# Scaling attention outputs instead of probabilities, with the inverse sums spread to rows by ScalarE and TensorE and the transposes copied by two engines

## The chip, the cores and the metric

The kernel runs on one core of a Trainium2 chip. The metric is the device time of one execution in microseconds (us). The core's engines work side by side, each through its own instructions in order: TensorE (PE, with its weight loads as PEld), VectorE (DVE), ScalarE (ACT), GpSimd (POOL) and SyncE (SP), which issues most DMAs. Matrix products and transposes are written to PSUM, from where another engine has to copy or read them.

## The reference

A trunk of two layers over 1024 tokens of 1024 features. Layer 0 mixes by a state-space scan and a convolution and is not touched. Layer 1 mixes by two kinds of attention, whose outputs are gated and multiplied by the output weights:

```python
def masked_softmax(s, mask):
    s = jnp.where(mask, s.astype(jnp.float32), NEG)
    m = jnp.max(s, axis=-1, keepdims=True)
    e = jnp.exp(s - m) * mask
    return e / jnp.maximum(jnp.sum(e, axis=-1, keepdims=True), 1e-30)
...
    p_c = masked_softmax(s_c, jnp.asarray(dist_c >= 0))
    o_cmp = jnp.einsum('bygsc,bcyd->bsygd', p_c, vc)
...
        o_sel = jnp.einsum('bygqk,byqkd->bqygd', p_s, vs)
...
        o_win = jnp.einsum('bygqk,bkyd->bqygd', p_w, vw)
...
    o = g[:, :, 0] * o_cmp + g[:, :, 1] * o_sel + g[:, :, 2] * o_win
```

This is NSA: 8 query heads on 2 key-value heads of 64 features, with three branches. The compressed branch attends to block averages (`vc` are their values), the selected branch to the blocks that rank highest by the compressed probabilities, the window branch to the last 512 tokens; `g` are sigmoid gates for each token, head and branch. MLA, the second kind, is ordinary causal attention of 8 heads of 64 value features with the same `masked_softmax`. Everything is in float32.

## The kernel before

Tokens lie in eight blocks `i` of 128 on the partitions. Layer 1 (`layer1`) goes through stages, of which three matter here. The order of the instructions on each engine is made by a scheduler from the code's data dependences and its own estimates, so that neighbouring loops overlap and an engine's order is not that of the code.

**Compression and gates.** `cmp_attn` (L1200) takes the compressed branch, block by block, in the free place `vslot` (`fr`): exponentials, sums, and at L1232 the probabilities times their gate, `pg`, into one of two places (by i % 2). TensorE transposes them (L1236), ScalarE copies them to `pcT` (L1238), and a DMA (L1239) stores `pcT` in `gp_dram`. For blocks 4 to 7 VectorE then ranks the key blocks (L1245 to L1261, a chain of small steps of which L1256 to L1260 each handle 128 x 512 elements), TensorE transposes the result (L1264), ScalarE casts it (L1267). In between run projections of the gates (`gate_proj`, products at L121, `th` at L1281 and L1282).

**NSA** (`nsa`, L1335). For each block, in the order 1, 2, 0, 3 to 7, and for each of two halves `gp` of four heads, first the window branch, then the selected branch: TensorE makes scores for 4, 2 or 1 heads at a time (L1385, mask, L1390) into one of two two-bank places `S`. `softmax_group` (L1286) takes the maximum (L1291, VectorE), the exponentials with their sums (L1294, ScalarE), the gate times the clamped inverse of the sums (L1300, L1301, VectorE), and multiplies the probabilities by it (L1303, VectorE). `transpose_group` (L1305) transposes them in 128 x 128 pieces, up to four into a PSUM bank (L1315), and ScalarE copies the bank to `PT` (L1316). The products with the values (L1405) of both branches, and that of `pcT` with `vc` (L1410), are summed in one bank `o`, the only one of its pool. `store_y` (L1326) multiplies it by the other gate (L1330).

**MLA** (`mla`, L1577) does the same for 16 steps of four heads: scores (L1603, L1606, L1607), `softmax_group`, `transpose_group` into `PTm`, products (L1615), `store_y`.

The float32 products appear in the trace as two records each, the transposes and the scores as one.

## Time and profile before

| | us |
|---|---|
| median of 3 runs | 1548.22 |
| lowest and highest | 1547.45, 1552.62 |
| profiled execution | 1549.67 |
| its span in the trace | 1547.9 |
| compression and gates | 807.7 to 921.5 |
| NSA | 921.5 to 1173.1 |
| MLA | 1173.1 to 1337.0 |

Over the span TensorE is busy for 1464.6 us (95%), VectorE for 962.6 (62%), ScalarE for 627.8 (41%), GpSimd for 375.4 (24%). Times in rows count from the start of the span. A row of the timeline gives the start, the length, and how many instructions of one kind follow one another (x8); records overlap, so the distance from one start to the next tells what an instruction costs. In brackets stands the idle time ahead of it and what ended that.

### The profile page before, as it was taken

Reading aid. Unit: us, or ns where it says so; the run is one execution under the profiler, and the core shown is the slowest. Engines: PE = TensorE matmul, PEld = TensorE weight load, DVE = VectorE, ACT = ScalarE, POOL = GpSimd, SP = SyncE. Lnnn points to the kernel's source line nnn. Section 1 sums busy time; section 2 is a strip of 40 time slices with the busy share of each in tenths; the row PEclk is TensorE's granted clock in tenths of the full one; section 3 lists DMA queues with packets and bytes.
Section 4 is the critical chain, followed back from the end, with each engine's and each line's share of the span. In section 5 each row is a group of like instructions: output and inputs, shape, how many; then the busy total and the mean of one; then the engine's idle time right before and its main releaser. Section 6 shows DMA issues by size and latency. Waiting matters only on the chain.

```text
span 1547.9 us, 22106 instructions
## 1 busy us (share of the span) xinstructions
PE 1464.6 (95%) x8284; PEld 1169.3 (76%) x8284; DVE 962.6 (62%) x1960; ACT 627.8 (41%) x1291; POOL 375.4 (24%) x334
## 2 busy tenths in 40 slices
PE   5879999989999999999999999999999999999998
PEld 4668878867787788789877776666666877787787
DVE  6799889968534655561386357787775676434322
ACT  4322312257213334431252237777665676312211
POOL 3369634331224201410321310010001100223400
PEclk8989999999999999999999999999999999999999
DMA  6232443323423422542833274221113241432422
GB/s 204 62 116 82 134 152 122 137 69 122 150 96 125 147 93 73 154 151 64 189 96 106 79 217 111 73 78 37 28 42 99 77 129 45 153 113 84 172 79 72
DMA packets 141475, 167.59 MB, mean 108 GB/s; under 512 B 20464, under 2 KB 108264, under 8 KB 141112
## 3 DMA queue, kind: packets, MB, share of 16 engines
q1 hardware_dynamic: 136440, 154.76, 32.5%
q0 software_dynamic: 4672, 11.39, 2.4%
q8 instruction: 66, 1.08, 0.3%
q14 instruction: 41, 0.34, 0.1%
q10 hardware_dynamic: 256, 0.03, 0.0%
HBM read 114.20 MB, written 49.94 MB: 106 GB/s over the span
## 4 chain that ended last, share of the span: by engine, by line
PE 74%; DVE 11%; ACT 4%; DMA 4%; issue 4%; POOL 2%; SPq 1%; ACTq 0%; DVEq 0%; POOLq 0%
PE S L121 41%; PE tr L1315 6%; PE tr L121 5%; PE o L1405 5%; PE o L1615 2%; PE S L1390 2%; PE S L1385 2%; PE S L1606 1%; PE S L1603 1%; PE S L1607 1%; DVE acc L544 1%; PE tr L849 1%; PE S L1320 1%; PE tr L1020 1%; DMA acc<-x 1%
## 5 line engine op out<-in xcount | busy, mean ns | idle before, releaser
L121 PE MATMUL S<-xT,wt 128*128 128x512 f32 x768 | 190.7, 402 | 12.3 <-DVE ext L267 10.0
L121 PE MATMUL S<-X,wt 128*128 128x512 f32 x768 | 183.6, 394 | 5.7 <-ACT wt L114 2.3
L121 PE MATMUL S<-wo,Y 128*128 128x512 f32 x768 | 181.7, 395 | 3.5 <-DVE gb L724 2.1
L121 PE MATMUL S<-wg,hT 128*128 128x512 f32 x720 | 173.6, 398 | 4.2 <-ACT wg L114 4.0
L121 PEld LDWEIGHTS S<-xT,wt 128*128 128x128 f32 x768 | 143.5, 191 | 44.2 <-DVE ext L267 10.5
L121 PEld LDWEIGHTS S<-wo,Y 128*128 128x128 f32 x768 | 143.6, 189 | 34.8 <-DVE gb L724 2.5
L121 PEld LDWEIGHTS S<-X,wt 128*128 128x128 f32 x768 | 141.8, 188 | 36.6 <-issue 3.7
L121 PEld LDWEIGHTS S<-wg,hT 128*128 128x128 f32 x720 | 134.9, 190 | 35.5 <-ACT wg L114 7.6
L1291 DVE TENSOR_REDUCE nm<-S 128x1 f32<-128x640 f32 (+7 forms) x132 | 128.9, 980 | 49.5 <-PE S L1390 30.1
L283 DVE SCALAR_TENSOR_TENSOR conv<-ext,conv 128x1024 f32<-128x1024 f32 x116 | 149.3, 1287 | 3.3
L115 POOL TENSOR_TENSOR wt<-raw,wt 128x1024 fp32r<-128x1024 f32 x34 | 84.2, 2492 | 99.8 <-ACT wt L114 99.6
L1294 ACT ACTIVATE pslot<-S,nm 128x640 f32<-128x640 f32 (+7 forms) x128 | 89.8, 708 | 31.7 <-DVE nm L1291 24.6
L1316 ACT COPY PT<-tr 128x512 f32<-128x512 f32 (+3 forms) x172 | 78.9, 492 | 40.9 <-PE tr L1315 36.1
L1405 PE MATMUL o<-PT,vslot 128*64 128x256 f32 x528 | 82.5, 391 | 0.4 <-ACT PT L1316 0.4
L1315 PE MATMUL tr<-ident,pslot 128*128 128x128 f32 x528 | 81.8, 283 | 0.0
L104 DVE TENSOR_SCALAR rs_v<-ss 128x1 f32<-128x1 f32 (+1 forms) x29 | 4.5, 154 | 116.9 <-ACT lh L100 102.3
L1315 PEld LDWEIGHTS tr<-ident,pslot 128*128 128x128 f32 x528 | 58.4, 142 | 24.9 <-issue 19.2
L1390 PE MATMUL S<-kst,qslot 112*128 112x512 f32 (+3 forms) x192 | 74.4, 400 | 0.0
L1385 PE MATMUL S<-kst,qslot 128*128 128x512 f32 (+3 forms) x192 | 70.3, 366 | 3.5 <-ACT pslot L1294 2.5
L834 POOL TENSOR_TENSOR lh<-lh 128x1024 f32<-128x1024 f32 x16 | 40.2, 2512 | 118.7 <-DVE lh L833 103.1
L100 ACT ACTIVATE lh<-S 128x1024 f32<-128x1024 f32 x16 | 16.4, 1027 | 125.6 <-issue 95.5
L899 DVE SCALAR_TENSOR_TENSOR ov<-ov,S 128x1024 f32<-128x1024 f32 (+1 forms) x17 | 19.7, 1158 | 72.6 <-issue 44.6
(452 smaller groups left out, 2759.2 us busy)
## 6 DMA issues: line engine op xcount, KB each, us to landing
h_dram<-lh POOLq DMA_DIRECT2D x16, 512.0 KB, 3.2
hr<-h_dram SPq DMA_DIRECT2D x14, 512.0 KB, 3.4
raw<-ev_w_in SPq DMA_DIRECT2D x16, 256.0 KB, 3.3
raw<-ev_w_in SPq DMA_DIRECT2D x8, 512.0 KB, 6.1
raw<-ev_w_out SPq DMA_DIRECT2D x8, 512.0 KB, 4.9
t<-ple_gate SPq DMA_DIRECT2D x8, 512.0 KB, 4.8
raw<-ple_gate SPq DMA_DIRECT2D x8, 512.0 KB, 4.4
lh<-x SPq DMA_DIRECT2D x8, 512.0 KB, 4.9
```

Source lines behind the costliest of these rows:

```text
L115: (eng or self.nc.gpsimd).tensor_tensor(lo, raw, hi, OP.subtract)
L121: self.nc.tensor.matmul(ps, l, r, start=n == 0, stop=n == len(seq) - 1)
L283: nc.vector.scalar_tensor_tensor(out=last if s == 30 else acc, in0=src, scalar=wc, in1=acc, op0=OP.mult, op1=OP.add)
L834: nc.gpsimd.tensor_tensor(hv, hv, xr, OP.add)
L1291: nc.vector.tensor_reduce(out=nm[:, 0:hg], in_=S[:, :, 0:n], op=OP.max, axis=AX.X, negate=True)
L1294: nc.scalar.activation(out=P[:, h, 0:n], in_=S[:, h, 0:n], func=AF.Exp, bias=nm[:, h:h + 1], accum_out=sm[:, h:h + 1])
L1315: nc.tensor.transpose(ps[:, c:c + 128], P[:, h, 128 * (k0 + k):128 * (k0 + k) + 128], self.ident)
L1316: nc.scalar.copy(PT[:, k0:k0 + n, s0:s0 + hg], ps[:, 0:128 * n * hg].rearrange("p (k h t) -> p k h t", h=hg, t=128))
L1385: nc.tensor.matmul(o_, QA[:, hd], KA[:, y, ks], start=True, stop=False)
L1390: nc.tensor.matmul(o_, qb[:, hd], KB[:, y, ks], start=False, stop=True)
L1405: nc.tensor.matmul(o[64 * y:64 * y + 64].rearrange("p g t -> p (g t)"), self.vsw[:, k0 + kt, 128 * br + 64 * y:128 * br + 64 * y + 64], PT ...
L1615: nc.tensor.matmul(o[64 * b:64 * b + 64, q], vm[:, kt, vs], PT[:, kt, 2 * b + q], start=(kt == 0), stop=(kt == nk - 1))
```

## The change

The probabilities are no longer scaled. `exp_group` is what is left of `softmax_group`: the maximum (L1297) and the exponentials (L1299), whose sums for all four heads of a branch go into one `sm`. The clamp, gate and inverse are made once for each branch and half (L1405, L1408) or MLA step, 48 times.

The inverse has to multiply the output, which has features on the partitions and tokens along a row. So `spread` (L1304, ScalarE) copies the four inverse sums to 64 columns each, and `inverse_rows` (L1309, TensorE) transposes that by two 128 x 128 transposes into PSUM; in NSA ScalarE copies the two branches' rows together to `f` (L1415). The two branches now have separate halves of the bank `o`; VectorE multiplies `o` by `f` (L1422), adds the branches (L1423) and adds the compressed output (L1424). In MLA the rows multiply the gate `sgm` in place (L1630), and `store_y` is as before.

The compressed branch is multiplied by its values in `cmp_attn` already (L1242, two products of 512 columns for each block). Its output `oc` is copied (L1244) into the place in which that block's `pg` was, and stored in `gp_dram` in place of `pcT` (L1245).

The copies of transposed probabilities (L1323) go alternately to ScalarE and VectorE: 132 and 126 of the 258.

```diff
+            ps = self.bank()
+            for y in range(2):
+                pr = slice(64 * y, 64 * y + 64)
+                nc.tensor.matmul(ps[pr], self.vc[pr], pcT[pr].rearrange("p g t -> p (g t)"), start=True, stop=True)
+            oc = fr[:, 4:8, 128 * (i % 2):128 * (i % 2) + 128]
+            nc.scalar.copy(oc, ps.rearrange("p (g t) -> p g t", g=4))
-            nc.sync.dma_start(self.gp_dram[i, :, 1], pcT)
+            nc.sync.dma_start(self.gp_dram[i, :, 1], oc)
...
-        nc.vector.reciprocal(r[:, 0:hg], r[:, 0:hg])
-        for h in range(hg):
-            nc.vector.tensor_scalar(out=P[:, h, 0:n], in0=P[:, h, 0:n], scalar1=r[:, h:h + 1], scalar2=None, op0=OP.mult)
+    def spread(self, r, dst):
+
+        self.nc.scalar.copy(dst, r.rearrange("p (a b o) -> p b a o", a=2, o=1).to_broadcast([128, 2, 2, 64]))
+
+    def inverse_rows(self, r, dst):
+
+        for b in range(2):
+            self.nc.tensor.transpose(dst[:, b], r[:, b].rearrange("p a e -> p (a e)"), self.ident)
...
-            nc.scalar.copy(PT[:, k0:k0 + n, s0:s0 + hg],
-                           ps[:, 0:128 * n * hg].rearrange("p (k h t) -> p k h t", h=hg, t=128))
+            copy = nc.vector.tensor_copy if (k0 // kb + s0 // hg) % 2 else nc.scalar.copy
+            copy(PT[:, k0:k0 + n, s0:s0 + hg], ps[:, 0:128 * n * hg].rearrange("p (k h t) -> p k h t", h=hg, t=128))
...
-                o = self.ps_o.tile([128, 2, 128], F32, tag="o", name="o")
+                o = self.ps_o.tile([128, 2, 2, 128], F32, tag="o", name="o")
+                r = self.t2([2, 2, 2, 64], name="inv")
...
+                    nc.vector.reciprocal(sm, sm)
+                    self.spread(sm, r[:, 1 - br])
+                    if br == 0:
+                        fp = self.bank().rearrange("p (b g t) -> p b g t", b=2, g=2)
+                        for b in range(2):
+                            self.inverse_rows(r[:, b], fp[:, b])
+                        f = self.t2([2, 2, 128], name="rows")
+                        nc.scalar.copy(f, fp)
...
-                for y in range(2):
-                    nc.tensor.matmul(o[64 * y:64 * y + 64].rearrange("p g t -> p (g t)"), self.vc[64 * y:64 * y + 64],
-                                     pcT[64 * y:64 * y + 64, 2 * gp:2 * gp + 2].rearrange("p g t -> p (g t)"),
-                                     start=False, stop=True, skip_group_check=True)
+                nc.vector.tensor_tensor(f, o, f, OP.mult)
+                nc.vector.tensor_tensor(f[:, 0], f[:, 0], f[:, 1], OP.add)
+                nc.vector.tensor_tensor(f[:, 0], f[:, 0], oc[:, 2 * gp:2 * gp + 2], OP.add)
...
+            f = self.bank()[:, 0:256].rearrange("p (g t) -> p g t", g=2)
+            self.inverse_rows(r, f)
+            nc.vector.tensor_tensor(sgm, f, sgm, OP.mult)
```

Three places show how the order on an engine changes. In the compression stage, TensorE's order around the first ranking transposition (L1264 before, L1270 after), for block 4; what stands in brackets is which engine or DMA queue an instruction waits for.

Before:

```order
L121 MATMUL S<-X_4494,wt 128x512 x4
L121 MATMUL S<-X_4495,wt 128x512 x4
L121 MATMUL S<-X_4494,wt 128x512 x2
L1264 MATMUL tr<-ident,pmv 16x128 [waits DVE_49,Activation_49]
L1264 MATMUL tr<-ident,pmv 16x128
L1236 MATMUL tr<-ident,vslot 128x128 [waits Activation_49]
L1236 MATMUL tr<-ident,vslot 128x128 x3
L121 MATMUL S<-X_4494,wt 128x512 x2
```

After:

```order
L121 MATMUL S<-X_4495,wt 128x512 x4
L1242 MATMUL tr<-pcT,vc 64x512 [waits Activation_49]
L1242 MATMUL tr<-pcT,vc 64x512
L1236 MATMUL tr<-ident,vslot 128x128 [waits DVE_49,PE_49]
L1236 MATMUL tr<-ident,vslot 128x128 x3
L1242 MATMUL tr<-pcT,vc 64x512 [waits Activation_49]
L1242 MATMUL tr<-pcT,vc 64x512
L1270 MATMUL tr<-ident,pmv 16x128 [waits DVE_49,PE_49]
L1270 MATMUL tr<-ident,pmv 16x128
L1236 MATMUL tr<-ident,vslot 128x128 [waits PE_49]
L1236 MATMUL tr<-ident,vslot 128x128 x3
L1242 MATMUL tr<-pcT,vc 64x512 [waits Activation_49]
```

The compressed products of blocks 3, 4 and 5 now stand around the transposition, that of block 4 right ahead of it, with no product of the gates between them.

VectorE's order at the same place, from the last ranking steps of block 4 (L1257 to L1261 before, L1263 to L1267 after).

Before:

```order
L1256 TENSOR_TENSOR E<-pmv 128x512 [waits DVE_49]
L1257 TENSOR_TENSOR E<-pmv 128x512
L1258 TENSOR_TENSOR E<-E,vslot 128x512 [waits DMAHW7_49,DVE_49]
L1259 TENSOR_TENSOR E<-E 128x512 [waits DVE_49]
L1260 TENSOR_REDUCE pmv<-E 128x32 [waits DVE_49]
L1261 TENSOR_SCALAR pmv<-pmv 128x32 [waits DVE_49]
L1232 TENSOR_TENSOR vslot<-E,cgt 128x2x4x64 [waits PE_49]
L1245 MEMSET pmv 128x2 [waits DVE_49]
```

After:

```order
L1263 TENSOR_TENSOR E<-pmv 128x512
L1232 TENSOR_TENSOR vslot<-E,cgt 128x2x4x64 [waits DMAHW0_49,Activation_49]
L1264 TENSOR_TENSOR E<-E,vslot 128x512 [waits DVE_49]
L1230 RECIPROCAL cgt<-ginv 128x8 [waits DVE_49]
L1232 TENSOR_TENSOR vslot<-E,cgt 128x2x4x64 [waits DMAHW1_49,Activation_49]
L1265 TENSOR_TENSOR E<-E 128x512 [waits DVE_49]
L1266 TENSOR_REDUCE pmv<-E 128x32 [waits DVE_49]
L1267 TENSOR_SCALAR pmv<-pmv 128x32 [waits DVE_49]
L1251 MEMSET pmv 128x2 [waits DVE_49,PE_49]
```

L1232 for blocks 5 and 6 stands inside the ranking of block 4, and waits for a DMA queue (that of `oc` of blocks 3 and 4) where it waited for TensorE.

TensorE's order at the start of NSA: before, from the second score tile's last head to the third's first; after, from the same head to the transposes of the first tile (`pslot`).

Before:

```order
L1385 MATMUL S<-kst,qslot 128x256
L1320 LDWEIGHTS mbf
L1320 MATMUL S<-mbf 128x128
L1390 MATMUL S<-kst,qslot 128x256
L1385 MATMUL S<-kst,qslot 128x256 [waits DVE_49,Activation_49]
```

After:

```order
L1326 MATMUL S<-mbf 128x128
L1399 MATMUL S<-kst,qslot 128x256
L1321 MATMUL tr<-ident,pslot 128x128 [waits Activation_49]
L1321 MATMUL tr<-ident,pslot 128x128
L1321 MATMUL tr<-ident,pslot 128x128 [waits Activation_49]
L1321 MATMUL tr<-ident,pslot 128x128
L1321 MATMUL tr<-ident,pslot 128x128 [waits Activation_49]
L1321 MATMUL tr<-ident,pslot 128x128
L1321 MATMUL tr<-ident,pslot 128x128 [waits Activation_49]
L1321 MATMUL tr<-ident,pslot 128x128
L1394 MATMUL S<-kst,qslot 128x256 [waits DVE_49]
```

The first tile's eight transposes, which followed the third score tile, now stand ahead of it, and each pair waits for its own exponential.

Over the whole order, runs of output products without another instruction between them become fewer: in NSA 74 (with the compressed products) become 64, in MLA 45 become 32, 26 of the latter with an odd number of products before and 20 after.

## Rows read from the trace of the kernel before

**Rows 1.** Windows: length, busy of PE, PEld, DVE, ACT, POOL, granted clock, DMA

```profile
807.70:921.50 113.80, 105.78 (x489) 86.26 (x488) 61.66 (x90) 28.64 (x45) 23.98 (x24) 1.00 0.42 125
921.50:1173.10 251.60, 247.78 (x1684) 164.66 (x1682) 181.81 (x425) 174.52 (x450) 16.33 (x29) 0.99 0.24 69
1173.10:1337.00 163.90, 159.34 (x1306) 126.39 (x1304) 107.83 (x233) 105.34 (x252) 12.40 (x10) 0.98 0.34 101
927.14:932.60 5.46, 5.46 (x25) 4.89 (x26) 3.79 (x13) 2.71 (x10) 0.37 (x2) 0.50 0.93 227
```

**Rows 2.** Waits of PE in NSA and MLA: total us, times, longest

```profile
PE S L1385 <- ACT pslot L1294: 2.5, 5, 1.4
PE S L1603 <- DVE sr L1301: 2.3, 1, 2.3
```

**Rows 3.** Groups by line: busy us, mean ns | idle before, releasers

```profile
L1303 DVE TENSOR_SCALAR pslot<-pslot,sr 128x640 f32<-128x640 f32 (+7 forms) x128 | 60.7, 500 | 2.9
L1315 PE MATMUL tr<-ident,pslot 128*128 128x128 f32 x528 | 81.8, 283 | 0.0
L1315 PEld LDWEIGHTS tr<-ident,pslot 128*128 128x128 f32 x528 | 58.4, 142 | 24.9 <-issue 19.2 <-ACT PT L1316 1.9 <-ACT pslot L1294 1.9
```

**Rows 4.** Timeline of PE in NSA: start, us, engine, line, operation

```profile
938.78 0.65 PE L1410 MATMUL o<-sgpc,vc 64*64 64x256 f32 x4
939.37 0.44 PE L1315 MATMUL tr<-ident,pslot 128*128 128x128 f32 x2
...
1017.74 0.65 PE L1405 MATMUL o<-PT,vslot 128*64 128x256 f32 x2
1018.32 0.76 PE L1315 MATMUL tr<-ident,pslot 128*128 128x128 f32 x5
```

**Rows 5.** Timeline of PE in MLA

```profile
1262.23 0.60 PE L1315 MATMUL tr<-ident,P 128*128 128x128 f32 x4
1262.76 1.09 PE L1615 MATMUL o<-PTm,vm 128*64 128x128 f32 x16
1263.79 0.44 PE L1603 MATMUL S<-KAm,qmslot 128*128 128x384 f32 x1
...
1268.98 0.66 PE L1615 MATMUL o<-PTm,vm 128*64 128x128 f32 x8
1269.57 0.87 PE L1315 MATMUL tr<-ident,P 128*128 128x128 f32 x6
1270.20 0.48 PE L1603 MATMUL S<-KAm,qmslot 128*128 128x512 f32 x1
```

**Rows 6.** Timeline of PE in compression and gates, waits in brackets

```profile
835.92 1.40 PE L121 MATMUL S<-X,wt 128*128 128x512 f32 x5 [1.59 <-DVE th L1282]
...
848.91 4.88 PE L121 MATMUL S<-X,wt 128*128 128x512 f32 x20 [1.14 <-ACT wt L114]
...
856.45 0.39 PE L1264 MATMUL tr<-ident,pmv 128*16 128x128 f32 x2 [2.65 <-DVE pmv L1261]
```

**Rows 7.** Timeline of DVE in the ranking of one block

```profile
845.32 1.07 DVE L1246 TENSOR_REDUCE pmv<-E 128x128 f32<-128x512 f32 x1 [5.15 <-issue]
...
849.05 2.89 DVE L1257 TENSOR_TENSOR E<-pmv 128x512 f32<-128x512 f32 x1
...
854.76 0.69 DVE L1259 TENSOR_TENSOR E<-E 128x512 f32<-128x512 f32 x1
```

**Rows 8.** Timeline of ACT behind a ranking transposition

```profile
845.31 0.57 ACT L1267 CAST sl<-tr 16x512 fp32r<-16x512 f32 x1 [10.81 <-PE tr L1264]
...
846.71 0.56 ACT L1238 COPY pcT<-tr 128x512 f32<-128x512 f32 x1
```

**Rows 9.** Landing of the stores of pcT issued at L1239

```profile
DMA to landing us min/median/max: 2.0/2.1/2.2
```

**Rows 10.** Timeline of PE at the start of NSA

```profile
929.97 1.91 PE L1315 MATMUL tr<-ident,pslot 128*128 128x128 f32 x8
931.53 0.56 PE L1385 MATMUL S<-kst,qslot 128*128 128x256 f32 x1
```

More of the change, by code (lines that the diff above doesn't have):

```diff
@@ L1284, in gate_proj, with exp_group @@
                 yield
-    def softmax_group(self, S, n, ginv, P):
+    def exp_group(self, S, n, P, sums):
         nc = self.nc
@@ L1291, in softmax_group @@
         nc.vector.tensor_reduce(out=nm[:, 0:hg], in_=S[:, :, 0:n], op=OP.max, axis=AX.X, negate=True)
-        sm = self.small.tile([128, 4], F32, tag="sm", name="sm", bufs=4)
         for h in range(hg):
             nc.scalar.activation(out=P[:, h, 0:n], in_=S[:, h, 0:n], func=AF.Exp, bias=nm[:, h:h + 1],
-                                 accum_out=sm[:, h:h + 1])
-        r = self.small.tile([128, 4], F32, tag="sr", name="sr", bufs=4)
-        if ginv is None:
-            nc.vector.tensor_scalar(out=r[:, 0:hg], in0=sm[:, 0:hg], scalar1=1e-30, scalar2=None, op0=OP.max)
-        else:
-            nc.vector.scalar_tensor_tensor(out=r[:, 0:hg], in0=sm[:, 0:hg], scalar=1e-30, in1=ginv, op0=OP.max, op1=OP.mult)
-        nc.vector.reciprocal(r[:, 0:hg], r[:, 0:hg])
-        for h in range(hg):
-            nc.vector.tensor_scalar(out=P[:, h, 0:n], in0=P[:, h, 0:n], scalar1=r[:, h:h + 1], scalar2=None, op0=OP.mult)
+                                 accum_out=sums[:, h:h + 1])
+    def spread(self, r, dst):
[3 more added lines that the diff above has]
+            self.nc.tensor.transpose(dst[:, b], r[:, b].rearrange("p a e -> p (a e)"), self.ident)
     def transpose_group(self, P, hg, nk, PT, s0):
@@ L1364, in nsa @@
             QA, qb, sp = cur
-            sgn, pcT = sp[:, 0], sp[:, 1]
+            sgn, oc = sp[:, 0], sp[:, 1]
             if self.Y[i // 2] is None:
@@ L1375, in nsa @@
                     PT = self.w16([8, 4, 128], F32, name="PT")
+                    sm = self.small.tile([128, 4], F32, tag="sm", name="sm", bufs=4)
                     for s0 in range(0, 4, hg):
@@ L1392, in nsa @@
                         np_ += 1
-                        gv = self.ginv[:, i, 8 * (br + 1):8 * (br + 2)].rearrange("p (y g) -> p y g", y=2)
-                        gv = gv[:, :, 2 * gp:2 * gp + 2]
-                        if hg == 4:
-                            gi = self.small.tile([128, 4], F32, tag="gv4", name="gv4")
-                            nc.gpsimd.tensor_copy(gi.rearrange("p (y g) -> p y g", y=2), gv)
-                        else:
-                            y, g2 = divmod(s0, 2)
-                            gi = gv[:, y, g2:g2 + hg]
@@ L1406, in nsa @@
                                              self.vsw[:, k0 + kt, 128 * br + 64 * y:128 * br + 64 * y + 64],
                                              PT[:, kt, 2 * y:2 * y + 2].rearrange("p g t -> p (g t)"),
-                                             start=(br == 1 and kt == 0), stop=False, skip_group_check=True)
-                for y in range(2):
-                    nc.tensor.matmul(o[64 * y:64 * y + 64].rearrange("p g t -> p (g t)"), self.vc[64 * y:64 * y + 64],
-                                     pcT[64 * y:64 * y + 64, 2 * gp:2 * gp + 2].rearrange("p g t -> p (g t)"),
-                                     start=False, stop=True, skip_group_check=True)
+                                             start=(kt == 0), stop=(kt == nk - 1), skip_group_check=True)
@@ L1593, in mla @@
             PT = self.w16([8, 4, 128], F32, name="PTm")
+            sm = self.small.tile([128, 4], F32, tag="sm", name="sm", bufs=4)
             for s0 in range(0, 4, hg):
@@ L1608, in mla @@
                 P = self.t4(name="P").rearrange("p (h n) -> p h n", h=hg)
-                self.softmax_group(S, n, None, P)
+                self.exp_group(S, n, P, sm[:, s0:s0 + hg])
                 self.transpose_group(P, hg, nk, PT, s0)
+            r = self.t2([2, 2, 64], name="inv")
+            nc.vector.tensor_scalar(out=sm, in0=sm, scalar1=1e-30, scalar2=None, op0=OP.max)
+            nc.vector.reciprocal(sm, sm)
+            self.spread(sm, r)
+            f = self.bank()[:, 0:256].rearrange("p (g t) -> p g t", g=2)
+            self.inverse_rows(r, f)
+            nc.vector.tensor_tensor(sgm, f, sgm, OP.mult)
             for q in range(2):
```

10 lines of the change are left out of this document (7 added, 3 removed).

## The prediction

> **What bounds the kernel now.** I read the stretches first, then TensorE's waits inside them, then single rows. [rows 1] cut the part of the run that the diff touches into three stages: compression and gates (807.7 to 921.5 us), NSA (921.5 to 1173.1) and MLA (1173.1 to 1337.0). TensorE is busy for 247.78 of 251.60 us in NSA and for 159.34 of 163.90 in MLA, at granted clocks of 0.99 and 0.98. VectorE has 181.81 and 107.83 us there, ScalarE 174.52 and 105.34. So what the change takes from VectorE or gives to ScalarE is worth something only where TensorE waits for it, and those waits are small: the two largest sums are 2.5 us for exponentials and 2.3 us for a reciprocal [rows 2], and the largest that a transposed copy causes is 1.9 us ahead of weight loads (PEld in [rows 3], with no idle time ahead of the transposes themselves). Compression is another matter: TensorE is busy for 105.78 of 113.80 us, so 8 us are idle, and VectorE (61.66) and ScalarE (28.64) are far from full; what stands idle there waits on a chain. The time therefore follows from how many TensorE instructions are added and removed, and from the chains in the compression stage.
>
> **What leaves VectorE, and why it is worth nothing by itself.** The 192 scalings at L1303 go: 128 in NSA for 60.7 us [rows 3] and 64 in MLA at like cost, 32. In their place VectorE gets 126 PSUM copies, which I price at ScalarE's 0.56 us for 512 columns [rows 8], 71 us, and 64 multiplies and adds of at most 0.69 us (L1259, a 512-column operation [rows 7]), 44 us. So it has at most some 22 us more over both stages, and still far less than TensorE. ScalarE loses those 126 copies (some 71 us) and gains 48 spreads and 24 copies of at most 0.56 us, 40 us. GpSimd, busy for 16.33 us in NSA [rows 1], loses the small copies of gates that went ahead of L1300. All stay covered by TensorE's 247.78 and 159.34 us, so I enter zero. If the cover were gone, the price is bounded by the waits in [rows 2, 3]: nobody can gain more than 2.5, 2.3 and 1.9 us from them. The first product of a group into the one output bank must now wait for the multiply at L1422, which itself waits for the copied rows (L1415); behind it on VectorE stand the maxima of the next score tile. In the order a score tile lies between the end of one group's products and the next group's first, so I count nothing; uncovered it would be 16 times 0.69, 11 us, which I hold unlikely. The Trainium skill, in TensorEngine Tiling (Array Packing), section PSUM Bottleneck, says to use both ScalarE and VectorE for PSUM evacuation, which the second copying engine does. By that rule the 1.9 us of [rows 3] would be the gain here; the row says that it cannot be more, and I enter zero.
>
> **TensorE's own work.** Durations are distances between starts, since records overlap.
> - *96 added transposes* (L1309; 64 in NSA, 32 in MLA). Six of them go from 1269.57 to 1270.20 [rows 5]: 0.105 each. 96 x 0.105 = **+10.1 us**.
> - *Compressed products leave NSA.* A run of 4 records (one pair at L1410) goes from 938.78 to 939.37 [rows 4], 0.59. There are 16: **-9.4 us**.
> - *They come back in compression* as 8 pairs of 512 columns (L1242). The price by columns: a run of 16 records (8 products of 128 columns) takes 1.03, one of 8 records 0.59 [rows 5], so four products cost 0.44, 0.11 each, and a run 0.15 beyond its columns. A pair of 512 columns is eight such products, 0.88. Transposes that stand ahead of a run take longer: four from 1262.23 to 1262.76 are 0.53 against 0.42 by the price above, 0.11 more. 0.88 + 0.15 + 0.11 = 1.14, eight times: **+9.1 us**. Columns alone would be 7.0; at NSA's rate (two runs of 0.59) 9.4.
> - *Fewer runs.* A run costs 0.15 + 0.11 = 0.26 beyond its columns. By the order, output products stand in 74 runs in NSA before and 64 after, and in 45 and 32 in MLA: 23 x 0.26 = **-6.0 us**. A lone product (two records) takes 0.58, from 1017.74 to 1018.32, as long as a pair's 0.59 [rows 4], so an odd run wastes a product; MLA has 26 odd runs before and 20 after: 6 x 0.11 = **-0.7 us**.
>
> Sum: +10.1 - 9.4 + 9.1 - 6.0 - 0.7 = **+3.1 us**. The bounds: -2.1 with compressed products at columns alone; +6 if long runs save nothing.
>
> **The new wait in the compression stage.** The output of the compressed product (oc) is written over the gated probabilities (pg) of the same block, and is read by its DMA. VectorE's L1232 for block i+2 writes that place and so has to wait for the landing. The order puts that L1232 ahead of the last three ranking steps (L1265 to L1267) of an earlier block, and VectorE runs in order; on TensorE the compressed product of block 4 stands right ahead of the ranking's transposition L1270 for block 4. The chain between the two has nothing beside it: copy of oc 0.56 (as pcT's [rows 8]), landing 2.1 (the old store's [rows 9]), L1232 0.69 (as L1259 at 854.76 [rows 7]), and the three steps, which before ran from 854.76 until the transposition started at 856.45 [rows 6, 7], 1.69: 5.0 us of idle TensorE. Beside it the products L1242 wait for pcT's copy: 0.56 once with nothing between, and once behind a cast, a gate activation and the copy, 845.31 to 847.27, 1.96 [rows 8], less the four transposes meanwhile (0.42): 1.5. Together 7.1 us. Against it stand three waits of before, 1.59, 1.14 and 2.65 us [rows 6], 5.4 together, at or behind this place: while TensorE stands still, VectorE, ScalarE and the weight loads catch up, so I let them go. Net **+1.7 us**, between -1.0 (the products' 2.1 hidden and the landing 0.6 quicker) and +7.1 (nothing relieved).
>
> **The start of NSA.** Before, the third score tile waits until 927.14 for exponentials (the longest, 1.4 us, of the five waits in the first of [rows 2]), and the eight transposes come later, 929.97 to 931.53, 1.56 us [rows 10]. After, the order has them ahead of that tile, and each pair waits for one exponential alone, so all but the last pair (0.2) falls into the wait: **-1.4 us**. The granted clock is 0.50 from 927.14 to 932.60 [rows 1], the lower of its two levels, after TensorE had stood idle; at full speed the 5.46 us there would be 2.73, so the bound below is -3.3 if the clock does not fall at all, and zero above.
>
> **Sum.** +3.1 + 1.7 - 1.4 = +3.4 us. The profiled execution took 1549.67, so its like would be 1553.1; that execution lies 1.45 above the median of 1548.22, which gives **1551.6 us**. A measurement of this kernel can tell 0.3%, 4.6 us, from no change: same is 1543.6 to 1552.9.
>
> **The rivals.**
> *A, slower: the waits add up and do not replace each other.* From the transposition of block 4 to that of block 5 TensorE has 28 products of the gates, 20 of which took 4.88 us at 848.91 [rows 6], so 6.8, with six transposes, a pair of L1242 and the 1.5 us ahead of it: 10 us. VectorE's chain for one block ran from 845.32 to 856.45, 11.1 us [rows 6, 7], but two of its steps filled 849.05 to 854.76; were they as quick as L1259, the chain would be 6.8, and 7.5 with an L1232 in it. For A: disturbed as it was there, it would be 11.8, longer than TensorE's 10, and then nothing is caught up. It decides from the point at which VectorE's chain between two ranking transpositions outlasts TensorE's work between them. Then the 5.4 us remain: +3.4 + 5.4 = +8.8, 1557.0 us.
> *B, faster: the chain of a softmax is what TensorE waits for.* Exponentials go straight to the transposes, so the 2.5 and 2.3 us of [rows 2] vanish, and the products moved into compression fill its 5.4 us of waits without new ones, since the landing is passed by other work: +3.1 - 5.4 - 4.8 = -7.1, 1541.1 us. Against it: the order leaves nothing between the product of block 4 and L1270.
> *C, slower: an added transpose costs its whole record.* A transpose's record is 0.283 us long [rows 3]; starts 0.105 apart [rows 5] hold where several follow each other, while the added ones come in pairs or fours. If each of the 96 cost its record: 96 x 0.178 = 17.1 us more, +20.5, 1568.7 us. Against it: four transposes alone took 0.53 up to the next start [rows 5], not 1.13. The Trainium skill, in TensorE: Matmul & The Clock Gate, section Part 4: PE-mode transpose, gives about 275 ns for a transposition in one kernel's context, set by access latency; by it alone 96 would be 26 us (estimate from that page). The trace agrees for one record but not for successive starts, 0.105 apart, hence 0.05.
>
> **How the numbers follow.** My forecast 0.50, A 0.30, B 0.15, C 0.05. Forecast counts as same (its +3.4 lies within 4.6), A and C as slower, B as faster: faster 0.15, same 0.50, slower 0.35. The range reaches over A with some 1 us to spare and below the forecast by the two bounds that can fall together (-2.1 at the columns, -1.9 at the clock, -2.7 at the chain): 1545.0 to 1558.0. B and C lie outside, 0.20.
>
> **What would show each step right or wrong.** In the profile after: NSA and MLA nearly full on TensorE as before, with 96 more transposes 0.10 to 0.11 us apart, and fewer, longer runs at L1635; VectorE busy no more than some 22 us longer than before; in compression one wait of about 5 us of L1270 behind L1267, with L1232 behind a landing just ahead of it on VectorE, and the three old waits gone (forecast) or still there (A). Wrong would be the whole sum if TensorE waited in NSA for the multiply at L1422 or for the copies at L1323, which no row of before shows, or if the clock fell after the 5 us wait: by the 5.46 us at 0.50 that would be about 2.7 us.

## The result and the profile after

The changed kernel takes 1568.26 us (median of 4 runs, 1565.83 to 1572.97) against 1548.64 for the kernel before (four runs by now): 1.0115 times as long, 95% interval 1.009 to 1.014. The forecast was 1551.6, the range 1545.0 to 1558.0. The profiled execution took 1567.31 us, with a span of 1565.5, 17.6 longer than before.

To see where these 17.6 us are I cut both traces at the same instructions: the gate product that waits for `kst` (810.21 before, 811.11 after), the first NSA score (921.50, 937.47) and the last output product of MLA. Windows, columns as in [rows 1]; before:

```profile
810.21:921.50 111.29, 104.74 (x480) 85.44 (x481) 59.21 (x87) 26.65 (x42) 23.98 (x24) 1.00 0.43 128
921.50:1336.95 415.45, 407.07 (x2986) 291.00 (x2984) 289.64 (x658) 279.86 (x702) 28.73 (x39) 0.98 0.28 82
```

After, and behind them three short stretches:

```profile
811.11:937.47 126.36, 117.05 (x516) 88.64 (x517) 55.05 (x87) 31.91 (x51) 23.05 (x24) 0.96 0.39 113
937.47:1353.60 416.13, 405.56 (x3006) 299.06 (x3004) 266.51 (x488) 254.57 (x640) 26.93 (x33) 0.98 0.29 81
844.10:854.30 10.20, 6.29 (x17) 3.66 (x18) 8.33 (x15) 2.54 (x4) 0.00 (x0) 0.50 0.31 84
1267.30:1274.10 6.80, 6.80 (x37) 6.28 (x35) 3.27 (x8) 3.50 (x13) 0.00 (x0) 0.50 0.76 235
1342.40:1345.80 3.40, 3.40 (x10) 2.62 (x10) 1.79 (x4) 1.42 (x4) 0.00 (x0) 0.51 0.85 281
```

Compression and gates are 15.1 us longer. NSA and MLA, from which the forecast took 7.4 us, are 0.7 longer. What stands ahead of the first cut and behind the last makes up 0.9 and 1.0. VectorE and ScalarE are less busy than before (266.51 and 254.57 us in NSA and MLA, against 289.64 and 279.86), so the change does what it says, and it gains nothing. TensorE's idle time, a row's length less its busy time, grows from 6.55 to 9.31 us in compression and from 8.38 to 10.57 in NSA and MLA. The short stretches are at TensorE's lower clock; before there was none in compression.

Where MLA begins, before and after, shows that NSA gained and MLA lost:

```profile
1173.88 0.22 PE L1603 MATMUL S<-KAm,qmslot 128*128 128x128 f32 x1
1184.61 0.22 PE L1616 MATMUL S<-KAm,qmslot 128*128 128x128 f32 x1
```

Up to there NSA took 252.4 us and takes 247.1; from there MLA took 163.1 and takes 169.0.

TensorE's waits in these stages, after (total us, times, longest):

```profile
PE tr L1321 <- ACT P L1299: 5.6, 4, 1.8
PE tr L1270 <- DVE pmv L1267: 5.4, 1, 5.4
PE tr L1242 <- ACT pcT L1238: 1.9, 2, 1.2
PE S L121 <- DVE kst L1063: 1.9, 1, 1.9
PE S L121 <- ACT wt L114: 1.9, 1, 1.9
PE S L1394 <- ACT pslot L1299: 1.7, 2, 1.5
```

Two are new and large: one of 5.4 us for the ranking in compression, and four together of 5.6 us for MLA's exponentials. Of the waits of [rows 6] the three are gone (a later one for weights grew from 1.17 to 1.9 us); those of [rows 2] too, except for 1.7 us.

TensorE around the first of them, in time order:

```profile
837.96 1.08 PE L1242 MATMUL tr<-pcT,vc 64*64 64x512 f32 x4
838.96 0.66 PE L1236 MATMUL tr<-ident,vslot 128*128 128x128 f32 x4
840.35 1.07 PE L1242 MATMUL tr<-pcT,vc 64*64 64x512 f32 x4 [0.73 <-ACT pcT L1238]
846.82 0.59 PE L1270 MATMUL tr<-ident,pmv 128*16 128x128 f32 x2 [5.39 <-DVE pmv L1267]
847.20 1.06 PE L1236 MATMUL tr<-ident,vslot 128*128 128x128 f32 x4
849.45 1.97 PE L1242 MATMUL tr<-pcT,vc 64*64 64x512 f32 x4 [1.19 <-ACT pcT L1238]
```

The pair of compressed products takes 1.01 us at 837.96 and 1.90 at 849.45, the four transposes 0.36 elsewhere and 1.06 at 847.20: both are at half speed behind the wait. With the 28 gate products that follow (7.85 us until 859.20, where 20 had taken 4.88 in [rows 6]) the low clock costs some 2.8 us here.

VectorE at the same time, and below it ScalarE's copy of the compressed output of block 4:

```profile
839.18 1.03 DVE L1252 TENSOR_REDUCE pmv<-E 128x128 f32<-128x512 f32 x1 [2.13 <-PE tr L1242]
...
844.44 0.69 DVE L1232 TENSOR_TENSOR vslot<-E,cgt 128x512 f32<-128x512 f32 x1 [0.56 <-DMA gp_dram<-vslot]
845.05 0.68 DVE L1265 TENSOR_TENSOR E<-E 128x512 f32<-128x512 f32 x1
845.77 0.69 DVE L1266 TENSOR_REDUCE pmv<-E 128x32 f32<-128x512 f32 x1
846.49 0.18 DVE L1267 TENSOR_SCALAR pmv<-pmv 128x32 f32<-128x32 f32 x1
...
841.47 0.58 ACT L1244 COPY vslot<-tr 128x512 f32<-128x512 f32 x1 [1.18 <-PE tr L1242]
```

The chain that the forecast named is there: the copy at 841.47, L1232 at 844.44 behind the landing, and the three steps behind that. But the landing holds VectorE up for only 0.56 us. The ranking had begun only at 839.18, after 2.13 us of waiting for a compressed product, and up to the landing its steps then follow each other with hardly a pause. So two chains of nearly one length end in one wait; the experiments take them apart.

### The profile page after: what moved, and what is told of

Its sections match the earlier page's. It is cut to its first block, busy times and chain, and to the rows that moved or that the text cites. A ratio compares the mean times of both kernels' runs of the same rounds, so it can differ in the third digit from the quotient of the medians.

```text
span 1565.5 us, 21926 instructions
## 1 busy us (share of the span) xinstructions
PE 1472.3 (94%) x8348; PEld 1179.5 (75%) x8348; DVE 935.7 (60%) x1790; ACT 607.3 (39%) x1237; POOL 371.4 (24%) x326
## 5 line engine op out<-in xcount | busy, mean ns | idle before, releaser
L121 PEld LDWEIGHTS S<-xT,wt 128*128 128x128 f32 x768 | 143.2, 191 | 44.5 <-DVE ext L267 10.5
L1297 DVE TENSOR_REDUCE nm<-S 128x1 f32<-128x640 f32 (+7 forms) x132 | 129.2, 980 | 51.1 <-PE S L1399 26.8
L1299 ACT ACTIVATE pslot<-S,nm 128x640 f32<-128x640 f32 (+7 forms) x128 | 89.4, 705 | 25.0 <-DVE nm L1297 21.3
L1321 PE MATMUL tr<-ident,pslot 128*128 128x128 f32 x528 | 77.5, 278 | 0.3 <-DVE PT L1323 0.2
L100 ACT ACTIVATE lh<-S 128x1024 f32<-128x1024 f32 x16 | 16.4, 1027 | 128.2 <-issue 96.0
L121 PE MATMUL tr<-wu,xT 128*128 128x256 f32 x384 | 54.3, 306 | 8.3 <-DVE xT L115 8.3
```

The source lines that it names most:

```text
L121: self.nc.tensor.matmul(ps, l, r, start=n == 0, stop=n == len(seq) - 1)
L1297: nc.vector.tensor_reduce(out=nm[:, 0:hg], in_=S[:, :, 0:n], op=OP.max, axis=AX.X, negate=True)
L1299: nc.scalar.activation(out=P[:, h, 0:n], in_=S[:, h, 0:n], func=AF.Exp, bias=nm[:, h:h + 1], accum_out=sums[:, h:h + 1])
L1321: nc.tensor.transpose(ps[:, c:c + 128], P[:, h, 128 * (k0 + k):128 * (k0 + k) + 128], self.ident)
```

## Experiments

For each run the table gives the median, the ratio to before in its own session (95% interval), and from its profile the two stages as cut above, in us. Before: 111.3 and 415.5.

| run | median | ratio | compression | NSA and MLA |
|---|---|---|---|---|
| after_again | 1566.85 | 1.0113 (1.0082 to 1.0143) | 129.5 | 414.8 |
| oc_over_pcT | 1565.80 | 1.0107 (1.0073 to 1.0142) | 127.0 | 414.2 |
| ranking_scratch_only | 1557.68 | 1.0070 (1.0046 to 1.0095) | 120.6 | 417.7 |
| ranking_buffers_apart | 1556.95 | 1.0054 (1.0039 to 1.0069) | 121.1 | 413.7 |
| cmp_in_nsa | 1567.01 | 1.0119 (1.0082 to 1.0157) | 111.3 | 431.7 |
| cmp_move_on_before | 1559.47 | 1.0069 (1.0053 to 1.0086) | 128.4 | 407.0 |
| copies_one_engine | 1583.03 | 1.0215 (1.0171 to 1.0259) | 128.2 | 428.2 |
| split_copies_on_before | 1549.35 | 1.0002 (0.9985 to 1.0019) | 112.6 | 412.9 |
| split_copies_nsa | 1554.31 | 1.0012 (0.9993 to 1.0031) | 112.9 | 414.5 |
| inverse_transposes_twice | 1581.05 | 1.0208 (1.0187 to 1.0229) | 126.5 | 430.5 |
| nsa_as_before | 1561.18 | 1.0049 (1.0030 to 1.0068) | 112.7 | 424.4 |
| mla_as_before | 1559.47 | 1.0052 (1.0034 to 1.0069) | 128.5 | 411.8 |
| wo_casts_on_gpsimd | 1572.59 | 1.0152 (1.0132 to 1.0172) | 128.0 | 405.7 |
| apart_mla_as_before | 1552.11 | 0.9999 (0.9985 to 1.0013) | 119.3 | 406.6 |
| scratch_apart_on_before | 1545.37 | 0.9980 (0.9969 to 0.9991) | 109.3 | 414.0 |

What stands ahead of the first cut, which no edit touches, took between 805.4 and 812.9 us in these profiles. So the stages of one profile can be compared with those of another, but not its whole span.

### What repeats

No edit:

> The changed kernel once more, to see which of its losses repeat. Its compression stage was 16.0 us longer than before (first NSA score at 937.47 against 921.51), with TensorE waiting 5.4 us for the ranking of block 4 and the granted clock at 0.50 from 845 to 855; NSA and MLA together were 415.9 against 415.3. Theory 1 (the time is lost in the compression stage: products 9, new waits 3 net, low clock 3): the 5.4 us wait and a low clock behind it stand there again, about 1568 us. Rival (the low clock comes by chance, and with it some 5 us): the low stretches stand at other places, and the time of the span differs by 3 us or more.

The waits of 5.39 us for the ranking and 5.6 for exponentials stand there to the hundredth, and the low stretches behind them too:

```profile
842.00:852.20 10.20, 5.92 (x16) 3.38 (x17) 8.12 (x17) 2.54 (x4) 0.00 (x0) 0.50 0.32 88
1265.20:1272.00 6.80, 6.80 (x36) 6.61 (x35) 3.62 (x7) 3.58 (x13) 0.04 (x1) 0.50 0.69 222
1340.30:1343.70 3.40, 3.40 (x13) 2.82 (x12) 2.29 (x4) 1.92 (x4) 0.34 (x1) 0.50 0.87 313
```

Both have one more at the start of MLA (6.8 us from 1192.2, 3.4 us from 1193.6), where before has one too (6.8 us from 1182.2). The rest differs: the first profile has a low stretch at 994, the second has them at 808 and at 893, the latter behind a wait of 1.9 us for weights that was there both times. So both executions lose clock behind the large waits, and behind one or two of the small ones that are not the same in both.

### The wait for the ranking

The compressed output over `pcT`, so that no L1232 waits for a landing:

```diff
-            oc = fr[:, 4:8, 128 * (i % 2):128 * (i % 2) + 128]
+            oc = pcT
```

> The changed kernel with one edit: the compressed output is written over pcT, in the buffer whose store every second block had to await already, and not over the gated probabilities, so that no L1232 waits for a landing. Theory 1: the wait of 5.4 us becomes at most 1.5 us, the clock behind it stays at 1.00, and 6 to 8 us of the 17.6 go: 1560 to 1562 us. Rival (the wait only gathers what other waits of the stage would take, or the low clock is not tied to it): 1 to 3 us go, 1565 to 1567.

Nothing of this: TensorE waits as long as in the changed kernel. Timeline of VectorE, and under it TensorE:

```profile
838.68 1.03 DVE L1252 TENSOR_REDUCE pmv<-E 128x128 f32<-128x512 f32 x1 [1.52 <-DMA gp_dram<-pcT]
...
844.58 0.59 PE L1270 MATMUL tr<-ident,pmv 128*16 128x128 f32 x2 [5.54 <-DVE pmv L1267]
```

The ranking's first step waits for a landing from `pcT`, although it reads nothing of it. Its scratch `pmv` is taken from the same pool of two buffers as `pcT`, and gets one only when both the compressed product of block 3 and, here, the store have let go of it. So a ranking that gets its buffer late is enough for the wait, without an L1232 behind a landing. The forecast had not asked what the added reader of `pcT` does to the next user of its pool. The next run moves `pmv` alone, into a place that lies free since the compressed scores were made, and leaves the output where the change has it:

```diff
-                pmv = self.t2((512,), name="pmv")
+                pmv = fr[:, 0]
```

> The changed kernel with the ranking's scratch (pmv) in a free place, the compressed output over the gated probabilities as in the change, so that L1232 still waits for its landing. If the landing chain makes the wait, as forecast (copy, landing, L1232, three steps, 5.0 us where the product of block 4 stands right ahead of the ranking's transposition), a wait of 3 to 5.5 us and the low clock behind it stay, 1563 to 1567 us. If the shared buffer makes it, the wait falls under 1.5 us and the time to that of both edits, 1557 us.

The wait is gone. TensorE:

```profile
836.24 1.08 PE L1242 MATMUL tr<-pcT,vc 64*64 64x512 f32 x4 [0.73 <-ACT pcT L1238]
837.24 0.39 PE L1270 MATMUL tr<-ident,vslot 128*16 128x128 f32 x2
838.78 0.63 PE L1236 MATMUL tr<-ident,vslot 128*128 128x128 f32 x4 [1.15 <-DVE vslot L1232]
```

The transposition L1270 follows the compressed product at once, and between 836 and 848 the granted clock is 1.00:

```profile
836.00:848.00 12.00, 9.63 (x46) 6.30 (x47) 11.23 (x24) 4.54 (x8) 0.00 (x0) 1.00 0.42 115
```

But the edit did more than free a buffer. With it the scheduler gave VectorE a new order: the last ranking step of block 4 now stands ahead of the L1232 of blocks 5 and 6, which had stood inside that ranking.

```profile
835.25 0.17 DVE L1267 TENSOR_SCALAR vslot<-vslot 128x32 f32<-128x32 f32 x1
837.95 0.69 DVE L1232 TENSOR_TENSOR vslot<-E,cgt 128x512 f32<-128x512 f32 x1
841.33 0.68 DVE L1232 TENSOR_TENSOR vslot<-E,cgt 128x512 f32<-128x512 f32 x1
```

So moving the scratch took both chains out of TensorE's way, and its run does not show that the landing costs nothing.

Both edits together:

> The changed kernel with two buffers of the compression stage taken apart: the compressed output over pcT (no L1232 waits for a landing), and the ranking's scratch (pmv) in a free place instead of one of the two buffers that it shared with pcT. In the changed kernel TensorE waited 5.4 us for the ranking of block 4; with only the first of these edits it still waited 5.5, since the ranking could start only when a buffer was given back. Theory 1 (both waits are chains of nearly one length, and the low clock from 842 to 852 follows the wait): the wait falls under 1.5 us, the low stretch goes, and the stage is 7 to 9 us shorter than the changed kernel's 137.6: about 1559 us. Rival (the stage's waits only move): stage within 3 us, 1565 us.

They give 1556.95 us, within the interval of the scratch alone. So the shared scratch is enough to make the wait, and moving it enough to end it. What the landing would cost by itself, in the order of the changed kernel, no run shows; since it ended last there, I take it to be about the same. The stage is 5 to 8 us shorter than in the changed kernel's two profiles (126.4, 129.5), and the whole 9 to 11 us, by ratios and by medians. The stage remains 9.8 us longer than before, of which the eight pairs of products at 1.01 us are 8.1.

### The compressed products moved

Into the stage, in the kernel before: the change's lines in `cmp_attn`, and in `nsa`

```diff
-                for y in range(2):
-                    nc.tensor.matmul(o[64 * y:64 * y + 64].rearrange("p g t -> p (g t)"), self.vc[64 * y:64 * y + 64],
...
+                f = self.t2([2, 128], name="rows")
+                nc.vector.tensor_tensor(f, o, oc[:, 2 * gp:2 * gp + 2], OP.add)
```

And back into NSA, in the changed kernel, with `pcT` stored as before:

```diff
+                cb = self.bank()[:, 0:256].rearrange("p (g t) -> p g t", g=2)
+                for y in range(2):
+                    nc.tensor.matmul(cb[64 * y:64 * y + 64].rearrange("p g t -> p (g t)"), self.vc[64 * y:64 * y + 64],
...
-                nc.vector.tensor_tensor(f[:, 0], f[:, 0], oc[:, 2 * gp:2 * gp + 2], OP.add)
+                nc.vector.tensor_tensor(f[:, 0], f[:, 0], cb, OP.add)
```

> The kernel before with one part of the change: the compressed products moved into the compression stage (output over the gated probabilities, one more addition on VectorE in NSA). Theory 1: the stage gets the 16 us of the changed kernel (products 8, waits 3, low clock 3), NSA loses 9 us of products: 5 to 8 us slower than before, 1554 to 1557. Rival (products moved into a stage with idle TensorE are free or nearly): 0 to 4 us faster.

> The changed kernel with the compressed products put back into NSA (32 products of 256 columns, into a PSUM bank of their own, since the output bank is scaled afterwards; pcT stored as before). Theory 1: the compression stage has its old length, 16 us less, and NSA gets 9.4 us of products and up to 2 us for shorter runs: 5 to 7 us less than the changed kernel, 1561 to 1563. Rival (the products cost the same anywhere and the waits of the stage come back in another form): within 2 us of the changed kernel.

In the kernel before, the stage becomes 17.1 us longer and NSA and MLA 8.5 shorter: 1559.47 us, 10.6 slower. That is the forecast's -9.4 and +9.1 with the wait of 5.4 us and its low clock on top, as in the changed kernel. The scratch was not moved in this version, so that it makes the wait here too is likely but not shown. Put back into NSA, in the changed kernel, the products cost as much as they did in compression: 15 us less there, 16 to 17 more here, of which 9.5 are the products, 4.7 more waits and some 2 shorter runs of the other products. My 5 to 7 us less did not come; the rival's case did. The parts of the change do not add: the move alone costs 10.6 us, the rest alone 18, both together 18.

### The copies

In the changed kernel all on ScalarE, in the kernel before on both engines, and there in NSA alone:

```diff
-            copy = nc.vector.tensor_copy if (k0 // kb + s0 // hg) % 2 else nc.scalar.copy
+            copy = nc.scalar.copy
```

> The changed kernel with all copies of transposed probabilities on ScalarE. Theory 1 (the copies are hidden on either engine): within 3 us of the changed kernel. Rival: the waits of 5.6 us for exponentials in MLA and the low clock there come from the new order that the two engines brought, so that they go and 4 to 6 us are saved. Opposite: ScalarE, which gets 126 copies of 0.5 us back, holds up the exponentials, 3 us or more lost.

> The kernel before with one part of the change: copies of transposed probabilities alternately on ScalarE and VectorE, scaling kept. Theory (TensorE hardly waits for copies before, so their engine is hidden): within 2 us of before. Rival (one engine cost 16 us in the changed kernel because of the order that came with it, so two engines gain as much where VectorE has room): 4 to 10 us faster. Opposite: VectorE, which keeps 192 scalings and gets 126 copies, becomes late for the maxima: 5 us or more slower.

> The kernel before with copies on two engines in NSA alone. With two engines in both stages the time did not change, but in the profile NSA and MLA together were 2.5 us shorter, NSA by 5 to 6 and MLA longer by 2 to 3, with new waits for copies at its end. If that is a property of the orders, NSA alone gives 3 to 6 us: 1543 to 1546. Rival (within the noise of one profile): 1548 to 1550.

In the kernel before the second engine changes nothing that can be measured, as the forecast entered it. In the changed kernel the one engine costs 16 us more. ScalarE is not full there (298.7 us busy of 428.2 in NSA and MLA). But the order has 114 runs of output products instead of 96, and 184 of transposes instead of 168, and TensorE is idle for 16.5 us instead of 10.6. Whether the order alone does this, or a ScalarE that is late at single steps, these runs do not separate. The 5 to 6 us that the profiles of the kernel before with two engines show as gained in NSA do not reach the whole time: with them in NSA alone it is 1.0012 of before, and 12 runs lie between 1545.5 and 1558.1. Part of that gain is the cut's, since MLA's first score stands ahead of NSA's last products in these two orders.

### The inverse transposes

```diff
-        for b in range(2):
+        for b in (0, 0, 1, 1):
```

> The changed kernel with each inverse transposition issued twice (192 instead of 96, the second writes the same). The added 96 stand right behind their like. By the forecast's price of 0.105 us they cost 10.1 us; by the 0.130 that the changed kernel's trace shows for a pair's share, 12.5; by a whole record of 0.28, 27. If the added ones fall into waits, 5 or less.

14 us. By distances between starts, with waits and low clock taken out, 192 take 23.0 us where 96 took 12.5: the second of each costs 0.109 us, close to the forecast's price, the first 0.130. The 96 stand in 42 places between other instructions, so most have no more than one like them beside them. The rest of the 14 are 3.6 us of waits and more runs. A whole record of 0.28, rival C's, is out.

### MLA

MLA's scaling as before within the change (`softmax_group` kept for MLA), and the reverse, the change's MLA and copies alone on the kernel before:

```diff
-                self.exp_group(S, n, P, sm[:, s0:s0 + hg])
+                self.softmax_group(S, n, None, P)
...
-            self.spread(sm, r)
-            f = self.bank()[:, 0:256].rearrange("p (g t) -> p g t", g=2)
-            self.inverse_rows(r, f)
-            nc.vector.tensor_tensor(sgm, f, sgm, OP.mult)
```

> The changed kernel with MLA's scaling as before (probabilities scaled by VectorE, no inverse transposes there; the copies still on two engines, NSA and compression changed). In the changed kernel MLA's 32 added transposes, its waits for exponentials (5.6 us in four places, absent before) and the low clock behind two of them lie in the last third. Theory 1 (the waits in MLA follow from transposes that the order now puts close behind the exponentials): waits for exponentials and the low stretches at 1267 and 1342 go, 5 to 9 us less than the changed kernel, 1558 to 1562. Rival (MLA's part costs only its 32 transposes, 4 us, and waits come in another form): 1564 or more.

> The kernel before with the change in MLA alone: outputs scaled there, inverse sums spread and transposed, copies on two engines in NSA and MLA; NSA's scaling and the compressed products as before. Theory 1: 32 transposes at 0.13, 4.2 us, waits of 5 us and low clock of 3 less fewer runs and the 2.3 us wait gone: 5 to 9 us slower than before, 1554 to 1558. Rival (what MLA loses comes only with NSA's change): within 3 us of before.

Without it the change is 7 to 10 us faster (by medians and by ratios), and it alone makes the kernel before 0.49% slower, 7.6 us (10.7 by the medians). In that kernel the waits for MLA's exponentials stand there again, without NSA's change:

```profile
PE tr L1334 <- ACT P L1312: 5.7, 4, 1.8
```

In the profile of the changed kernel with MLA as before they are gone, and the low stretch at 1267 with them. But other waits came:

```profile
935.58:1347.40 411.82, 401.09 (x2987) 295.25 (x2986) 293.48 (x592) 249.40 (x624) 27.08 (x33) 0.99 0.30 82
1190.00 0.41 PE L1634 MATMUL S<-KAm,qmslot 128*128 128x384 f32 x1 [2.42 <-DMA qmslot<-qm_dram]
1340.02 0.73 PE L121 MATMUL S<-wo,Y 128*128 128x512 f32 x2 [1.19 <-ACT wo L114]
1342.20 0.73 PE L121 MATMUL S<-wo,Y 128*128 128x512 f32 x2 [1.45 <-ACT wo L114]
1344.14 3.51 PE L1646 MATMUL o<-PTm,vm 128*64 128x128 f32 x30 [1.20 <-DVE PTm L1342]
```

A low stretch of 3.4 us stands from 1344.3, and TensorE is idle for 10.7 us of the two stages, as in the changed kernel. They are 3.0 to 4.3 us shorter than there: 32 transposes at 0.13 us are gone and the clock is low for less time, while 12 products that the change had moved into the last stage are back. So the time came as expected, but the part of the rival that waits come in another form is true as well, and some 4 of the 7 to 10 us are MLA's own transposes.

TensorE in the changed kernel, then ScalarE at the same time:

```profile
1264.30 0.43 PE L1635 MATMUL o<-PTm,vm 128*64 128x128 f32 x2
1266.53 1.24 PE L1321 MATMUL tr<-ident,P 128*128 128x128 f32 x8 [1.79 <-ACT P L1299]
...
1263.38 1.99 ACT L114 CAST wo<-raw 128x1024 fp32r<-128x1024 f32 x2 [2.43 <-PE S L1616]
1265.28 1.11 ACT L1299 ACTIVATE P<-S,nm 128x1024 f32<-128x1024 f32 x1
```

Since no scaling stands between exponential and transpose any more, the order has the transposes close behind the scores, and one product alone in between. ScalarE meanwhile casts the output weights for 2.0 us, and the exponential comes behind that. The same rows stand at 1341.41. Before, MLA's transposes hardly waited, as those of NSA in [rows 3]:

```profile
L1315 PE MATMUL tr<-ident,P 128*128 128x128 f32 x288 | 43.0, 283 | 0.1
```

To see what this costs, the casts of that half of the weights go to GpSimd:

```diff
-            self.parts(wt[:, 0, ks], wt[:, 1, ks], raw, self.nc.vector if mix and q else None)
+            if hi is None:
+                self.parts(wt[:, 0, ks], wt[:, 1, ks], raw, self.nc.vector if mix and q else None)
+            else:
+                hi.tensor_copy(wt[:, 0, ks], raw)
+                self.nc.gpsimd.tensor_tensor(wt[:, 1, ks], raw, wt[:, 0, ks], OP.subtract)
```

> The changed kernel with the casts of the first half of the output weights, which ScalarE and VectorE make during MLA, on GpSimd. In the changed kernel TensorE waits 1.79 us at 1266.5 and at 1341.4 for an exponential that stands behind two such casts (2.0 us) on ScalarE, and the granted clock is 0.50 behind both. If that is MLA's loss: both waits go with the low stretches, 4 to 8 us less, 1559 to 1563 us. Rival (the transposes and the other waits are the loss): within 2 us of the changed kernel, 1565 to 1568.

As a whole it is slower. The last stage takes 228.3 us where the changed kernel's takes 211.9: TensorE is idle there for 18.9 us instead of 9.6, 6.3 of them waits for the rest of the weights, and the clock is low for 10.2 us around the longest. But up to the end of MLA the run shows the mechanism:

```profile
936.90:1342.55 405.65, 396.81 (x2997) 292.15 (x2996) 261.32 (x485) 248.82 (x634) 33.14 (x38) 1.00 0.28 78
1262.56 1.09 PE L1326 MATMUL tr<-ident,P 128*128 128x128 f32 x8 [0.23 <-ACT P L1304]
...
1359.12 2.07 PE L121 MATMUL S<-wo,Y 128*128 128x512 f32 x4 [4.42 <-ACT wo L114]
```

The wait of 1.79 us is 0.23, the one at 1341 too, both low stretches are gone (clock 1.00 in the row of the two stages), and NSA and MLA take 405.65 us, 10.5 less than in the changed kernel's first profile and 9.1 less than in its second. The two waits give 3.1 us of that together; the low clock behind them, at half speed for 10.2 us, some 5. Nine products that moved on to the last stage are some 1.6 us of it and no gain.

### Both repairs, and a version below both kernels

> The changed kernel with both repairs: the buffers of the compression stage apart (10 us less in its own run) and MLA's scaling as before. If the parts add up, 1550 to 1553: the products moved (+10) against fewer products and waits in NSA (-6). Rival (the repaired waits come back elsewhere): 1556 or more. Below before, 1545, only if NSA's gain is larger than its run with the buffers apart shows.

```profile
808.09:927.40 119.31, 113.82 (x516) 87.00 (x517) 51.85 (x86) 31.43 (x51) 23.18 (x24) 1.00 0.38 119
927.40:1333.95 406.55, 397.79 (x2987) 292.81 (x2986) 293.31 (x592) 249.43 (x624) 27.10 (x33) 1.00 0.29 83
```

0.9999 of before. The two repairs add up (1.0113 less 0.0059 and 0.0061 would be 0.9993): 8.0 us more in compression, 8.9 less in NSA and MLA. What is left of the change is even with the kernel before. The clock of 1.00 in both rows is that of one execution of 1547.13 us, well below the median of 1552.11.

The scratch moved in the kernel before, nothing else:

> The kernel before with the ranking's scratch in a free place and nothing else. Before, TensorE waits 2.65 us for the ranking of block 6, with products of the gates ahead of it. If the scratch is what makes the ranking late, that wait goes: 2 to 4 us faster, 1545 to 1547. Rival (the ranking is late by its steps that took 2.9 and 2.8 us in place of 0.7): no change.

0.998, interval 0.9969 to 0.9991, 1545.37 us: some 3 us faster than before, and faster than both kernels. The wait of 2.65 us of [rows 6] is gone; 0.89 is left at the first ranking:

```profile
832.45 0.38 PE L1264 MATMUL tr<-ident,vslot 128*16 128x128 f32 x2 [0.89 <-DVE vslot L1261]
```

## Why the prediction was wrong

By stages the forecast was +10.8 us in compression, where +15.1 were measured, -7.4 in NSA and MLA, where it was +0.7, and nothing elsewhere, where it was +1.9. Three steps failed: the "I enter zero" for the edges of VectorE and ScalarE, above all in MLA; the prices of the added transposes and of fewer runs; and the low clock behind the new wait, which had no term in the sum.

**What bounds the kernel.** That TensorE does, was right. That what VectorE and ScalarE save is worth nothing by itself, too: they are less busy by 23 and 25 us in NSA and MLA (the forecast had VectorE up to 22 us busier), and the two stages are no shorter. Wrong was the conclusion "I enter zero" for what happens at their edges. The waits of before bound what can be gained from them; they are no bound on what a new order can make TensorE wait for. This is the step that failed in MLA. The two waits that the prediction did name, for the multiply at L1422 and for the copies at L1323, came to 0.4 us together.

**TensorE's own work**, with waits and low clock taken out. Products out of NSA -9.4 (measured 9.3), into compression +9.1 (eight pairs at 1.01 us: 8.1). The 96 transposes: 12.5 instead of 10.1, 0.130 each, as they stand in pairs and fours, where my row had six in a line. Fewer runs: -6.7, measured about -4.6 over all products, scores and old transposes. Sum +3.1 forecast, +6.7 measured. (The order also moved 12 other products from NSA and MLA into the last stage, some 2.4 us.)

**The new wait.** Its size and the chain that I priced were right, term by term: the copy at 841.47, L1232 at 844.44, TensorE at 846.82, 5.39 us against 5.0. But a second chain ran beside it, to within 0.56 us of the same length, which I did not see: `pmv` takes its buffer from the pool of `pcT`. That is why the wait looked explained in the first profile, and why taking the landing away changed nothing. The waits for `pcT`'s copies were right (2.1 forecast, 1.9), and so was that the three waits of before go (5.4), though a later one grew by 0.7. Not in the sum was the low clock behind the wait, 2.8 us, which the last part of the prediction names at 2.7 as a thing that would make it wrong.

**The start of NSA.** Right: the wait at the third score tile is gone and the low stretch with it, which was the bound of -3.3 rather than -1.4. A wait of 1.52 us at 992.72 took part of it back.

**MLA.** Not foreseen at all: 5.6 us of waits for exponentials, with low clock behind two of them. The forecast for MLA's terms was -0.7 (transposes +3.4, fewer runs -4.1), and MLA became 6 us longer. Taking those two waits alone away gave some 8 us. Rival B had put a gain there (the 2.3 us of [rows 2], which did go), and the order turned the shorter chain into new waits.

**The rivals.** A (the waits add up) ended at 1557.0 with the right sign, but its mechanism did not happen: the old waits were relieved. C's 1568.7 came within 0.5 us of the measured time by luck: the second transposes at 0.109 us and the first at 0.130 exclude its price.

Taken together, the forecast of +3.4 us missed by 14: 4.3 in compression, 8.1 in NSA and MLA, 1.9 elsewhere. Moving the ranking's scratch gives back 7 to 11 us (of which the forecast had 1.7, net of the old waits), MLA's scaling as before 7 to 10 with its transposes, and both together the whole loss. What stays open is how MLA's loss divides between waits, clock and runs, since no edit takes one of them alone, what the landing costs without the shared scratch, and the 1 to 2 us of compression that I can't place.

## To carry to other kernels

When an operation gets a new reader or a longer life, look for every other user of its pool: the next one to draw a buffer waits for it, on an engine that has nothing to do with the data. When a wait has the size that you priced, ask whether a second chain ends at the same place before you call it explained. A chain that gets shorter is worth nothing if the scheduler answers by putting its consumer closer: look in the new order for what stands between producer and consumer on the waiting engine, and what else stands in the producer's queue. And price a wait of TensorE with the clock behind it, where the trace shows low stretches behind waits.

## What the runs showed of the hardware

TensorE's granted clock fell to its lower level in or behind the waits: 0.50 for 10.2 us around the wait of 5.39 us in both profiles of the changed kernel, some 2.8 us lost, and not there when the wait was gone; 0.50 for 6.8 and 3.4 us behind two waits of 1.79, some 5 us lost, and not there when these were 0.23. Not each wait did so: behind one of 1.21 us at 1250.91 there was none, behind one of 1.9 at 893 in one profile of two. The executions of one kernel spread by several us, roughly with the mean granted clock: of 12 runs of `split_copies_nsa` the five up to 1549.9 us have 0.981 to 0.985, the seven from 1553.7 to 1558.1 us 0.979 to 0.982. Its one profile, at 1545.66, lies 9 us off its median.
